# A two-layer hybrid trunk on one core: the third FFN column pair computed plainly, the norm's residual additions and sums of squares on VectorE, and a gate product placed ahead of the second gates

## The chip, the cores and the metric

The kernel runs on one core of a Trainium2 chip. The metric is the device time of one execution in microseconds (us). The engines are called as in the profile: PE is TensorE, PEld its weight loads, DVE is VectorE, ACT is ScalarE, POOL is GpSimd, SP is SyncE, which issues most loads.

## What is computed

A two-layer causal decoder trunk on 512 tokens of width 1024, float32 in and out. Layer 0 mixes with dilated attention and an S5 state-space block side by side; layer 1 mixes with a Griffin block (a convolution of width 4, block-diagonal gates, a linear recurrence, a GELU branch). Each mixer and each FFN stands between two RMS norms, and the second norm's output is added to the residual:

```python
def rms_norm(x, g):
    y = x32 * lax.rsqrt(jnp.mean(x32 * x32, axis=-1, keepdims=True) + NORM_EPS) * g
def swiglu(x, w_gate, w_up, w_down):
    return (jax.nn.silu(x @ w_gate) * (x @ w_up)) @ w_down
...
    x = x + rms_norm(mixer(rms_norm(x, g_mix_pre)), g_mix_post)
    x = x + rms_norm(swiglu(rms_norm(x, g_ffn_pre), ...), g_ffn_post)
```

(The last two lines are put in short form.) The FFN's hidden width is 2816, which is 22 blocks of 128 columns.

## The kernel before

The residual lies transposed in eight tiles `xT` of 128 features by 512 tokens. Products are made in float32 quality from three products of split operands: high by high, low by high, high by low (`mm3`, recorded as L170). Activations and weights are therefore split into a high part (a copy on ACT) and a low part (a subtraction on DVE); for weights these are L240 and L241, tiles `whi_*` and `wlo_*`.

**The norm.** `out_proj` (L416) makes an output projection and the two norms behind it. It is used three times: `mo0` (layer 0's mixer, ahead of its FFN), `fd0` (layer 0's FFN, ahead of layer 1's mixer) and `mo1` (layer 1's mixer, ahead of its FFN). `norm_half` (L478) handles one half of the tokens: `col_sums` adds squares over the features on PE (`cs`), `rstd_of` makes the reciprocal root, `bcast_row` spreads it over the partitions on PE (`bc`). Then for each of eight features: gain by row on DVE (L496, tile `o_*`), the residual addition (L500 on DVE for the first feature, L502 on POOL for the other seven), the high part `xh` on ACT (L503), the square `nsq` on ACT (L506), and later the low part `xl` on DVE (L491). `next_sums` (L470) adds these squares over the features on PE into `ns`, the sum for the next pre-norm: 32 matmuls of 128x1 per norm, which a trace shows as 64 rows. While a norm runs, `half_cols` (L555) already multiplies the first four columns of the next product, feature by feature (`mo0b`, `fd0b`, `mo1b`); one feature of one half is twelve 256-wide matmuls. The next pre-norm's factor is applied after the products, so it can come late.

**The FFN's columns.** `ffn_up` (L598) computes gate and up columns in pairs. Pairs 0 and 1 are the four plain columns begun in the norm. Pairs 2 to 21 use a Strassen-like scheme on 2x2 blocks, with 84 matmuls of 256 columns in place of 48 of 512. It needs transformed weights (`pair_weights`, L636: four additions, seven splits into high and low) and transformed activations `t1` to `t4` (L657 to L677, from `xa` and `xb`); `t1` is written over the second halves of `xh` and `xl`. The products are named by block, `f00b` to `f03b` in layer 0 and `f10b` to `f13b` in layer 1.

**Layer 1's mixer.** `odd_body` (L1484): four plain columns from the norm (`fd0b`), four more (`xbb`), the convolution (`xc`), gates (`rg` on PE, `gr` and `gi` on ACT, L1557), the recurrence (L1561; exponentials and roots on ACT, multiplications and a scan on DVE), and the branch `gate_product` (L1580, 24 matmuls of 512 columns each, tile `gg`), whose GELU times the recurrence gives `y1h` and `y1l` (L1596, L1597), the operands of `op_mo` in `mo1`. Lines 1601 to 1613 set the order of gates, recurrences and gate products.

**What sets the order.** A tile scheduler with a time model orders each engine's instructions; inside the norm `seq_of` and `pin` keep the written order of a half. A heap of generators (`start`, `step_one`, `tick`, `drain`) puts the norm's steps between matmuls by due times (NORM_CS, NORM_BC, NORM_F). Loads are issued on SP's queue in order, each when its buffer is free.

Of the kernel before, what the change touches and what calls it, by code (L numbers as in the profile page):

```python
# [19 lines left out]
P = 128  # L20
S = 512
# [73 lines left out]
def hybrid_trunk(  # L95
# [320 lines left out]
    def out_proj(wget, ks, yh, yl, pname, layer, nm, otile, gname, glayer, ntail, tail_alloc, early, eng0=None,  # L416
# [44 lines left out]
        xh, xl = xg_tiles(nm)  # L461
        acc2 = [None, None]
        ready.clear()
# [14 lines left out]
        def norm_half(h):  # L478
            def srcs(t):
                return [acc[:, t * P:(t + 1) * P], acc2[h][:, t % 2 * P:(t % 2 + 1) * P]]  # L480

            yield NORM_CS[h]
            cs = col_sums(srcs, 2 * h, 2, f"{nm}{h}")
            r = rstd_of(cs, 2, f"{nm}{h}", seq_of, None if eps is None else eps[:, 2 * h:2 * h + 2])
            yield NORM_BC[h]
            row = bcast_row(r, 2, f"{nm}{h}")
            late = []

            def split_lo():
                f = late.pop(0)  # L490
                seq_of(dve.scalar_tensor_tensor(xl[f][:, HS[h]], xT[f][:, HS[h]], col(gname, glayer * NF + f),  # L491
                                                xh[f][:, HS[h]].bitcast(F32), op0=ALU.mult, op1=ALU.subtract))

            for f in range(NF):
                oh, xf = o[f][:, HS[h]], xT[f][:, HS[h]]
                seq_of(dve.scalar_tensor_tensor(oh, oh, col(pname, layer * NF + f), row, op0=ALU.mult, op1=ALU.mult))  # L496
                if late and late[0] < max(NDVE, f - 1):
                    split_lo()
                if f < NDVE:
                    seq_of(dve.tensor_tensor(xf, xf, oh, op=ALU.add))  # L500
                else:
                    pool.tensor_tensor(xf, xf, oh, op=ALU.add)  # L502
                seq_of(act.activation(xh[f][:, HS[h]], xf, AF.Copy, scale=col(gname, glayer * NF + f)))  # L503
                if f % 2 == 0:
                    q = sb.tile([P, S], F32, tag="sqacc" if h else "sq", bufs=2, name=f"nsq_{nm}{h}{f}")
                seq_of(act.activation(q[:, HS[f % 2]], xf, AF.Square))  # L506
                late.append(f)
                if f % 2 and f > 1:
                    next_sums(h, (f - 3, f - 2), qlast)
                if f % 2:  # L510
                    qlast = q
                ready.update((h, q) for q in range(late[0]))
                yield NORM_F
            next_sums(h, (NF - 2, NF - 1), qlast)
            while late:
                split_lo()
            ready.update((h, q) for q in range(NF))
# [20 lines left out]
        drain()  # L538
        in_order[0] = False
        sets["main"].insert(0, nb)  # L540
        return xh, xl, (first, bs), nsum
# [7 lines left out]

    NFIRST = 4  # L550

    def first_cols(lst, nm, eng=None):
# [17 lines left out]

    def gemm_cols(lst, first, xh, xl, nm, evac):

# [7 lines left out]
        for i in range(NFIRST, len(lst)):  # L580
            w2 = wcols(lst[i][0], lst[i][1], NF, f"{nm}{i}")
            b = bank(f"{nm}b{i}")
            for k in range(NF):
                mm3(b, w2(k), xh[k], xl[k], k == 0, k == NF - 1)
            w2.free()
            evac(i, b)
# [11 lines left out]
    def ffn_up(layer, xh, xl, first, nsum, nm, hp):  # L598
# [32 lines left out]

        heads = gemm_cols(cols2[:NFIRST], first, xh, xl, nm, evac)
        next(heads)
# [15 lines left out]

        own = iter([*range(11, NH), 3, 4, 5, 6])  # L650
        for q in range(NFIRST // 2 + 3):
            retired.add((hp, f"hh{q}"))
        wa, wc, wd, wb = pair_weights(
            NFIRST // 2, lambda name: hp.tile([P, S], F32R, tag=f"hh{next(own)}", name=name), sb)


        t1 = [(xh[k][:, HS[1]], xl[k][:, HS[1]]) for k in range(HK)]  # L657
        th, tl = [], []
        for k in range(HK):
            a = hp.tile([P, S], F32, tag=f"hh{7 + k % 2}", name=f"xa_{nm}{k}")  # L660
# [3 lines left out]
            raw = Raw(4, HT, f"tr_{nm}{k}")  # L664
            (t2, t3), (t4, t0) = [(t[:, 0], t[:, 1]) for t in raw.parts]
            dve.tensor_tensor(t0, a[:, HS[1]], a[:, HS[0]], op=ALU.subtract)
# [4 lines left out]
            l = hp.tile([P, 3, HT], F32R, tag="tq", bufs=8, name=f"tl_{nm}{k}")  # L671
            for src, hi, lo in ((raw.parts[0], h[:, 0:2], l[:, 0:2]), (t4, h[:, 2], l[:, 2]), (t0, *t1[k])):
                act.activation(hi, src, AF.Copy)
                dve.tensor_tensor(lo, src, hi.bitcast(F32), op=ALU.subtract)
            raw.free()
            th.append(h)
            tl.append(l)  # L677
        for _ in heads:
            pass
        give([(hp, f"hh{q}") for q in range(7, NH)])  # L680
        X = {
# [11 lines left out]

        for n in range(NFIRST // 2, NH):
            if n > NFIRST // 2:
                for q in range(n + 3):
# [787 lines left out]
    def odd_body(xh, xl, first, nsum, lp):  # L1484
# [119 lines left out]
        recurrence(range(NF // 2))  # L1604
        gg += [gate_product(1), gate_product(2)]
        gates(2, last["sqrt"])
        gates(3, last["sqrt"])
        gg.append(gate_product(3))
        recurrence(range(NF // 2, NF))
# [61 lines left out]
```

## Time and profile before

| what | value |
|---|---|
| median of 3 runs | 1168.26 us (1167.83 to 1178.44) |
| the profiled execution | 1169.77 us, span 1167.7 us |
| mean granted PE clock of that execution | 0.990 |
| PE busy | 1131.7 us (97%), 7550 matmul rows |
| DVE busy | 876.8 us (75%), 1841 instructions |
| ACT busy | 626.6 us (54%) |
| POOL busy | 60.6 us (5%) |

Times in the rows are microseconds from the start of the span. A row of a chain gives start, length and the work that the end waited for. A row of a timeline gives start, length, engine, line, operation, output and inputs, and in brackets the idle time before it with what ended it. A row of the waits names the waiting engine and line, what released it, and the time in all, the number of waits and the longest. Groups of back-to-back instructions overlap in their ends, so the price of one in a row is the distance of starts rather than the length.

### The profile page before, as it was taken

To read this page: it belongs to the slowest core of one execution; us is meant where nothing else is said; L and a number is where in the kernel's file an instruction comes from. 1 tells how busy PE (TensorE), PEld (TensorE's weight loads), DVE (VectorE), ACT (ScalarE), POOL (GpSimd) and SP (SyncE) were. 2 spreads that over 40 slices of the span, in tenths; PEclk is the share of its full clock that TensorE was granted. 3 is DMA by queue.
4 is the path that set the end of the run, shared out by engine and by line. 5 is a ranking of instruction groups with operands and counts; after the bars stand their busy time and mean duration, and the time that the engine had idled before them with its cause. 6 is when DMAs were issued, how large, how long until landed. Compare 5 with 4: busy or idle time off the path is not lost.

```text
span 1167.7 us, 20255 instructions
## 1 busy us (share of the span) xinstructions
PE 1131.7 (97%) x7550; PEld 1013.2 (87%) x7550; DVE 876.8 (75%) x1841; ACT 626.6 (54%) x1290; POOL 60.6 (5%) x100
## 2 busy tenths in 40 slices
PE   6999899999999999999999999999999999999997
PEld 6877666889999999988889887889999999988886
DVE  7989675478999899882345887956999899984224
ACT  7556576357655555652244479744855455582221
POOL 1000010003000000000004000004000000000001
PEclk9999989999999999999999999999999999999999
DMA  8534410522333332423330323430253333334221
GB/s 211 144 117 134 108 45 1 172 64 63 93 109 100 101 99 83 125 92 96 121 100 1 106 86 98 126 109 1 77 146 95 101 109 91 90 119 126 91 63 72
DMA packets 165561, 113.45 MB, mean 97 GB/s; under 512 B 26852, under 2 KB 142296, under 8 KB 165464
## 3 DMA queue, kind: packets, MB, share of 16 engines
q1 hardware_dynamic: 162168, 109.95, 32.2%
q10 hardware_dynamic: 3040, 2.17, 0.7%
q8 instruction: 59, 0.97, 0.3%
q14 instruction: 38, 0.31, 0.1%
q0 software_dynamic: 256, 0.06, 0.0%
HBM read 103.75 MB, written 4.19 MB: 92 GB/s over the span
## 4 chain that ended last, share of the span: by engine, by line
PE 82%; DVE 5%; ACT 5%; DMA 4%; issue 2%; POOL 0%; ACTq 0%; DVEq 0%; POOLq 0%; SPq 0%
PE fo L170 10%; PE op_fd L170 10%; PE op_mo L170 6%; PE f00b L170 5%; PE f02b L170 5%; PE f01b L170 4%; PE f11b L170 4%; PE f10b L170 4%; PE f12b L170 4%; PE qkv L170 4%; PE gg L170 3%; PE f03b L170 2%; PE f13b L170 2%; PE mo1b L170 2%; PE mo0b L170 2%; PE xbb L170 2%
## 5 line engine op out<-in xcount | busy, mean ns | idle before, releaser
L241 DVE TENSOR_TENSOR wlo_fo<-wraw_fo,whi_fo 128x512 fp32r<-128x512 f32 x44 | 30.3, 691 | 63.8 <-PE fo L170 58.7
L170 PE MATMUL op_fd<-hi_f,whi_fd 128*128 128x512 f32 (+1 forms) x200 | 73.7, 369 | 0.0
L170 PE MATMUL op_fd<-lo_f,whi_fd 128*128 128x512 f32 (+1 forms) x200 | 73.4, 367 | 0.0
L170 PE MATMUL op_fd<-hi_f,wlo_fd 128*128 128x512 f32 (+1 forms) x200 | 73.0, 367 | 0.0
L170 PE MATMUL fo<-wlo_fo,hi_f 128*128 128x512 f32 x176 | 69.4, 394 | 0.0
L170 PE MATMUL fo<-whi_fo,lo_f 128*128 128x512 f32 x176 | 69.1, 394 | 0.0
L170 PE MATMUL fo<-whi_fo,hi_f 128*128 128x512 f32 x176 | 68.9, 396 | 0.0
L240 ACT ACTIVATE whi_fo<-wraw_fo 128x512 fp32r<-128x512 f32 x44 | 27.6, 631 | 70.6 <-DMA wraw_fo<-in_ffn_w_down_dram 43.4
L241 DVE TENSOR_TENSOR wlo_fd<-wraw_fd,whi_fd 128x512 fp32r<-128x512 f32 x44 | 30.1, 690 | 46.4 <-ACT whi_fd L240 42.5
L240 ACT ACTIVATE whi_fd<-wraw_fd 128x512 fp32r<-128x512 f32 x44 | 27.4, 629 | 54.7 <-DMA wraw_fd<-in_ffn_w_down_dram 33.8
L170 PEld LDWEIGHTS op_fd<-lo_f,whi_fd 128*128 128x128 f32 x200 | 37.7, 189 | 6.8
L170 PEld LDWEIGHTS op_fd<-hi_f,wlo_fd 128*128 128x128 f32 x200 | 37.7, 189 | 6.7
L170 PEld LDWEIGHTS op_fd<-hi_f,whi_fd 128*128 128x128 f32 x200 | 37.7, 189 | 6.6
L170 PE MATMUL qkv<-whi_qkv,xh_m 128*128 128x512 f32 x96 | 40.5, 427 | 0.0
L170 PEld LDWEIGHTS fo<-whi_fo,lo_f 128*128 128x128 f32 x176 | 33.1, 188 | 7.8
L170 PEld LDWEIGHTS fo<-whi_fo,hi_f 128*128 128x128 f32 x176 | 33.1, 188 | 7.7
L170 PEld LDWEIGHTS fo<-wlo_fo,hi_f 128*128 128x128 f32 x176 | 33.1, 188 | 7.5
L170 PE MATMUL qkv<-wlo_qkv,xh_m 128*128 128x512 f32 x96 | 38.3, 399 | 0.0
L170 PE MATMUL qkv<-whi_qkv,xl_m 128*128 128x512 f32 x96 | 38.0, 396 | 0.0
L644 DVE TENSOR_TENSOR wraw_s_f<-wraw_f,wraw_f 128x512 f32<-128x512 f32 x40 | 27.4, 684 | 11.4 <-DMA wraw_f<-in_ffn_w_up_dram 10.7
L241 DVE TENSOR_TENSOR wlo_mo<-wraw_mo,whi_mo 128x512 fp32r<-128x512 f32 x32 | 21.4, 686 | 14.5 <-ACT whi_mo L240 14.2
L645 DVE TENSOR_TENSOR wraw_t_f<-wraw_s_f,wraw_f 128x512 f32<-128x512 f32 x40 | 27.3, 682 | 6.0 <-DMA wraw_f<-in_ffn_w_gate_dram 6.0
(1974 smaller groups left out, 4297.8 us busy)
## 6 DMA issues: line engine op xcount, KB each, us to landing
wraw_f<-in_ffn_w_gate_dram SPq DMA_DIRECT2D x88, 256.0 KB, 3.1
wraw_f<-in_ffn_w_up_dram SPq DMA_DIRECT2D x88, 256.0 KB, 3.3
wraw_fd<-in_ffn_w_down_dram SPq DMA_DIRECT2D x44, 256.0 KB, 2.8
wraw_fo<-in_ffn_w_down_dram SPq DMA_DIRECT2D x44, 256.0 KB, 2.9
wraw_qkv<-in_ev_w_in_dram SPq DMA_DIRECT2D x24, 256.0 KB, 3.5
wraw_mo<-in_ev_w_out_dram SPq DMA_DIRECT2D x16, 256.0 KB, 4.3
wraw_xb<-in_od_w_in_dram SPq DMA_DIRECT2D x16, 256.0 KB, 2.8
wraw_gg<-in_od_w_in_dram SPq DMA_DIRECT2D x16, 256.0 KB, 2.8
```

The source lines that it names most:

```text
L170: self.pin(nc.tensor.matmul(o, lhsT=lhsT, rhs=rhs, start=start, stop=stop, **kw))
L240: act.activation(hi, src, AF.Copy)
L241: eng.tensor_tensor(lo, src, hi.bitcast(F32), op=ALU.subtract)
L644: dve.tensor_tensor(s1, a21, a22, op=ALU.add)
L645: dve.tensor_tensor(s2, s1, a11, op=ALU.subtract)
```

## The change

Three edits. First, a third pair of FFN columns is plain (`NPLAIN = 3`): `gemm_cols` gets two more columns, `f0b4` and `f0b5`, with weights `f0p4` and `f0p5`; the scheme begins with pair 3, and `t1` is put over `xh` and `xl` only after the plain columns. Second, in the norm all residual additions are on DVE, the squares go to a ring of half tiles, DVE adds them up, and PE makes four totals of 128x1 at the end. Third, the gate product of feature 3 is written ahead of the third and fourth gate blocks.

```diff
--- before.py
+++ after.py
@@ -459,7 +459,8 @@
             o.append(t)
         first = early()
         xh, xl = xg_tiles(nm)
-        acc2 = [None, None]
+        acc2, total = [None, None], [None, None]
+        on_dve = True
         ready.clear()


@@ -485,6 +486,11 @@
             yield NORM_BC[h]
             row = bcast_row(r, 2, f"{nm}{h}")
             late = []
+            if on_dve:
+
+                sq = [sb.tile([P, S], F32, tag="sqacc" if h else "sq", bufs=2, name=f"nsq_{nm}{h}{i}")
+                      for i in range(2)]
+                sq = [q[:, HS[i]] for q in sq for i in range(2)]

             def split_lo():
                 f = late.pop(0)
@@ -494,24 +500,33 @@
             for f in range(NF):
                 oh, xf = o[f][:, HS[h]], xT[f][:, HS[h]]
                 seq_of(dve.scalar_tensor_tensor(oh, oh, col(pname, layer * NF + f), row, op0=ALU.mult, op1=ALU.mult))
-                if late and late[0] < max(NDVE, f - 1):
+                if late and (on_dve or late[0] < max(NDVE, f - 1)):
                     split_lo()
-                if f < NDVE:
+                if on_dve or f < NDVE:
                     seq_of(dve.tensor_tensor(xf, xf, oh, op=ALU.add))
                 else:
                     pool.tensor_tensor(xf, xf, oh, op=ALU.add)
                 seq_of(act.activation(xh[f][:, HS[h]], xf, AF.Copy, scale=col(gname, glayer * NF + f)))
-                if f % 2 == 0:
-                    q = sb.tile([P, S], F32, tag="sqacc" if h else "sq", bufs=2, name=f"nsq_{nm}{h}{f}")
-                seq_of(act.activation(q[:, HS[f % 2]], xf, AF.Square))
                 late.append(f)
-                if f % 2 and f > 1:
-                    next_sums(h, (f - 3, f - 2), qlast)
-                if f % 2:
-                    qlast = q
+                if on_dve:
+                    seq_of(act.activation(sq[f % 3] if f else sq[3], xf, AF.Square))
+                    if f > 1:
+                        seq_of(dve.tensor_tensor(sq[3], sq[3], sq[(f - 1) % 3], op=ALU.add))
+                else:
+                    if f % 2 == 0:
+                        q = sb.tile([P, S], F32, tag="sqacc" if h else "sq", bufs=2, name=f"nsq_{nm}{h}{f}")
+                    seq_of(act.activation(q[:, HS[f % 2]], xf, AF.Square))
+                    if f % 2 and f > 1:
+                        next_sums(h, (f - 3, f - 2), qlast)
+                    if f % 2:
+                        qlast = q
                 ready.update((h, q) for q in range(late[0]))
                 yield NORM_F
-            next_sums(h, (NF - 2, NF - 1), qlast)
+            if on_dve:
+                seq_of(dve.tensor_tensor(sq[3], sq[3], sq[(NF - 1) % 3], op=ALU.add))
+                total[h] = sq[3]
+            else:
+                next_sums(h, (NF - 2, NF - 1), qlast)
             while late:
                 split_lo()
             ready.update((h, q) for q in range(NF))
@@ -537,6 +552,10 @@
         bs = half_cols(0, first, xh, xl, None, nm)
         drain()
         in_order[0] = False
+        if on_dve:
+            for t in range(NT):
+                pe.matmul(nsum[:, t:t + 1], lhsT=total[t // 2][:, t % 2 * P:(t % 2 + 1) * P], rhs=ones[:, 0:1],
+                          start=True, stop=True)
         sets["main"].insert(0, nb)
         return xh, xl, (first, bs), nsum

@@ -548,6 +567,7 @@
         return dve.scalar_tensor_tensor(l, src, g, h.bitcast(F32), op0=ALU.mult, op1=ALU.subtract)

     NFIRST = 4
+    NPLAIN = 3

     def first_cols(lst, nm, eng=None):
         return [wcols(w, c0, NF, f"{nm}{i}", base=sb, eng=eng) for i, (w, c0) in enumerate(lst[:NFIRST])]
@@ -568,7 +588,7 @@
                 tick()
         return bs

-    def gemm_cols(lst, first, xh, xl, nm, evac):
+    def gemm_cols(lst, first, xh, xl, nm, evac, ready_w=None):

         ws, bs = first
         half_cols(1, ws, xh, xl, bs, nm)
@@ -578,7 +598,7 @@
         for i in range(NFIRST):
             evac(i, bs[i])
         for i in range(NFIRST, len(lst)):
-            w2 = wcols(lst[i][0], lst[i][1], NF, f"{nm}{i}")
+            w2 = ready_w(i) if ready_w else wcols(lst[i][0], lst[i][1], NF, f"{nm}{i}")
             b = bank(f"{nm}b{i}")
             for k in range(NF):
                 mm3(b, w2(k), xh[k], xl[k], k == 0, k == NF - 1)
@@ -629,7 +649,7 @@
                 act.activation(env[n][1], b, AF.Copy)
                 gated(*env[n], n)

-        heads = gemm_cols(cols2[:NFIRST], first, xh, xl, nm, evac)
+        heads = gemm_cols(cols2[:2 * NPLAIN], first, xh, xl, nm, evac, lambda i: plain[i - NFIRST])
         next(heads)
         mid()

@@ -647,36 +667,47 @@
             dve.tensor_tensor(s4, a12, s2, op=ALU.subtract)
             return [Chunk(t, f"{nm}{n}{q}", alloc=alloc) for t, q in ((r0, "a"), (rs, "c"), (r1, "d"), (rt, "b"))]

-        own = iter([*range(11, NH), 3, 4, 5, 6])
-        for q in range(NFIRST // 2 + 3):
+        own = iter(range(11, NH))
+        for q in range(NPLAIN + 3):
             retired.add((hp, f"hh{q}"))
-        wa, wc, wd, wb = pair_weights(
-            NFIRST // 2, lambda name: hp.tile([P, S], F32R, tag=f"hh{next(own)}", name=name), sb)
+        plain = [Chunk(Raw(NF, P, f"{nm}p{i}", cols2[i][0][:, cols2[i][1]:cols2[i][1] + P].rearrange(
+            "(k p) n -> p k n", p=P), base=sb), f"{nm}p{i}",
+            alloc=lambda name: hp.tile([P, S], F32R, tag=f"hh{next(own)}", name=name))
+            for i in range(NFIRST, 2 * NPLAIN)]


         t1 = [(xh[k][:, HS[1]], xl[k][:, HS[1]]) for k in range(HK)]
         th, tl = [], []
+        z = Raw(HK, HT, f"tz_{nm}")
+        z0 = [z.parts[k // z.step][:, k % z.step] for k in range(HK)]
         for k in range(HK):
             a = hp.tile([P, S], F32, tag=f"hh{7 + k % 2}", name=f"xa_{nm}{k}")
             b = hp.tile([P, S], F32, tag=f"hh{9 + k % 2}", name=f"xb_{nm}{k}")
             act.activation(a, xT[k], AF.Copy, scale=col("g1", layer * NF + k))
             act.activation(b, xT[k + HK], AF.Copy, scale=col("g1", layer * NF + k + HK))
             raw = Raw(4, HT, f"tr_{nm}{k}")
-            (t2, t3), (t4, t0) = [(t[:, 0], t[:, 1]) for t in raw.parts]
+            (t2, t3), (t4, _) = [(t[:, 0], t[:, 1]) for t in raw.parts]
+            t0 = z0[k]
             dve.tensor_tensor(t0, a[:, HS[1]], a[:, HS[0]], op=ALU.subtract)
             dve.tensor_tensor(t3, b[:, HS[1]], a[:, HS[1]], op=ALU.subtract)
             dve.tensor_tensor(t2, b[:, HS[1]], t0, op=ALU.subtract)
             dve.tensor_tensor(t4, t2, b[:, HS[0]], op=ALU.subtract)
             h = hp.tile([P, 3, HT], F32R, tag="tq", bufs=8, name=f"th_{nm}{k}")
             l = hp.tile([P, 3, HT], F32R, tag="tq", bufs=8, name=f"tl_{nm}{k}")
-            for src, hi, lo in ((raw.parts[0], h[:, 0:2], l[:, 0:2]), (t4, h[:, 2], l[:, 2]), (t0, *t1[k])):
+            for src, hi, lo in ((raw.parts[0], h[:, 0:2], l[:, 0:2]), (t4, h[:, 2], l[:, 2])):
                 act.activation(hi, src, AF.Copy)
                 dve.tensor_tensor(lo, src, hi.bitcast(F32), op=ALU.subtract)
             raw.free()
             th.append(h)
             tl.append(l)
+        wa, wc, wd, wb = pair_weights(NPLAIN)
         for _ in heads:
             pass
+
+        for k in range(HK):
+            act.activation(t1[k][0], z0[k], AF.Copy)
+            dve.tensor_tensor(t1[k][1], z0[k], t1[k][0].bitcast(F32), op=ALU.subtract)
+        z.free()
         give([(hp, f"hh{q}") for q in range(7, NH)])
         X = {
             "11": [(xh[k][:, HS[0]], xl[k][:, HS[0]]) for k in range(HK)],
@@ -691,8 +722,8 @@
             for k in range(HK):
                 mm3(o[:, HS[0]], w2(k0 + k), x[k][0], x[k][1], k == 0 and not onto, k == HK - 1, skip_group_check=onto)

-        for n in range(NFIRST // 2, NH):
-            if n > NFIRST // 2:
+        for n in range(NPLAIN, NH):
+            if n > NPLAIN:
                 for q in range(n + 3):
                     retired.add((hp, f"hh{q}"))
                 places[:] = [p for p in places if p not in retired]
@@ -1602,10 +1633,9 @@
         gates(1)
         gg = [gate_product(0)]
         recurrence(range(NF // 2))
-        gg += [gate_product(1), gate_product(2)]
+        gg += [gate_product(1), gate_product(2), gate_product(3)]
         gates(2, last["sqrt"])
         gates(3, last["sqrt"])
-        gg.append(gate_product(3))
         recurrence(range(NF // 2, NF))
         for f in range(NF):
             gated(f, gg[f])
```

How the instructions move, at three places. The first is DVE in the first half of the norm `mo0`; `o_mo` is the projection, `xT` the residual, `xl` the low part, `nsq` the squares. Before:

```order
L496 SCALAR_TENSOR_TENSOR o_mo04_2932<-o_mo04_2932,cols_143,bc_mo00_3125 128x256
L491 SCALAR_TENSOR_TENSOR xl_mo02_2998<-xT_2_149,cols_143,xh_mo02_2990 128x256
L380 TENSOR_SCALAR rst_mo01_3216<-cs_mo01_3211 128x2
L496 SCALAR_TENSOR_TENSOR o_mo05_2934<-o_mo05_2934,cols_143,bc_mo00_3125 128x256
L491 SCALAR_TENSOR_TENSOR xl_mo03_2999<-xT_3_150,cols_143,xh_mo03_2991 128x256
L496 SCALAR_TENSOR_TENSOR o_mo06_2936<-o_mo06_2936,cols_143,bc_mo00_3125 128x256
L491 SCALAR_TENSOR_TENSOR xl_mo04_3000<-xT_4_151,cols_143,xh_mo04_2992 128x256
```

and in the change:

```order
L502 SCALAR_TENSOR_TENSOR o_mo05_2934<-o_mo05_2934,cols_143,bc_mo00_3125 128x256
L497 SCALAR_TENSOR_TENSOR xl_mo04_3000<-xT_4_151,cols_143,xh_mo04_2992 128x256
L506 TENSOR_TENSOR xT_5_152<-xT_5_152,o_mo05_2934 128x256
L514 TENSOR_TENSOR nsq_mo001_3129<-nsq_mo001_3129,nsq_mo000_3128 128x256
L502 SCALAR_TENSOR_TENSOR o_mo06_2936<-o_mo06_2936,cols_143,bc_mo00_3125 128x256
L497 SCALAR_TENSOR_TENSOR xl_mo05_3001<-xT_5_152,cols_143,xh_mo05_2993 128x256
L506 TENSOR_TENSOR xT_6_153<-xT_6_153,o_mo06_2936 128x256
L514 TENSOR_TENSOR nsq_mo001_3129<-nsq_mo001_3129 128x256
```

Two operations per feature have become four, and the split follows one feature behind the gain instead of two.

The second place is PE in the second half of `mo0`, where the squares' sums (`ns_mo`) stood among the first columns (`mo0b`). Before:

```order
L170 MATMUL mo0b0_3161<-xh_mo01_2989,whi_f00_0_2944 128x256
L474 MATMUL ns_mo0_3004<-ones_131,nsq_mo014_3351 128x1 x2
L170 MATMUL mo0b0_3161<-xh_mo01_2989,wlo_f00_0_2945 128x256
L170 MATMUL mo0b1_3162<-xh_mo01_2989,whi_f01_0_2956 128x256
L170 MATMUL mo0b1_3162<-xh_mo01_2989,wlo_f01_0_2957 128x256
L170 MATMUL mo0b2_3163<-xh_mo01_2989,whi_f02_0_2968 128x256
L474 MATMUL ns_mo0_3004<-ones_131,nsq_mo014_3351 128x1 x2
```

and in the change, at the end of that half, with the third plain pair (`f0b5`) behind it:

```order
L170 MATMUL mo0b3_3165<-xh_mo07_2995,wlo_f03_1_2985 128x256
L170 MATMUL ns_mo0_3004<-ones_131,nsq_mo011_3277 128x1 x2
L170 MATMUL mo0b0_3162<-xl_mo07_3003,whi_f00_1_2948 128x256
L170 MATMUL mo0b1_3163<-xl_mo07_3003,whi_f01_1_2960 128x256
L170 MATMUL mo0b2_3164<-xl_mo07_3003,whi_f02_1_2972 128x256
L170 MATMUL mo0b3_3165<-xl_mo07_3003,whi_f03_1_2984 128x256
L170 MATMUL f0b5_3654<-xh_mo00_2988,whi_f0p5_0_3495 128x512
L170 MATMUL f0b5_3654<-xl_mo00_2996,whi_f0p5_0_3495 128x512
```

A norm had eleven such groups of two or four matmuls; it now has two of two, one for each half.

The third place is PE in layer 1's mixer, at the last gate (`rg1_7`). Before:

```order
L170 MATMUL rg1_7_8616<-ch6_8220,wlo_rg3_1_8585 128x512
L170 MATMUL rg1_7_8616<-ch7_8269,whi_rg3_1_8584 128x512
L170 MATMUL rg1_7_8616<-cl7_8270,whi_rg3_1_8584 128x512
L170 MATMUL rg1_7_8616<-ch7_8269,wlo_rg3_1_8585 128x512
L170 MATMUL gg3_8638<-xh_fd00_7434,whi_gg3_0_8630 128x512
L170 MATMUL gg3_8638<-xl_fd00_7442,whi_gg3_0_8630 128x512
```

and in the change:

```order
L170 MATMUL gg4_8618<-xh_fd03_7354,whi_gg4_0_8610 128x512
L170 MATMUL rg1_7_8554<-ch6_8119,whi_rg3_1_8522 128x512
L170 MATMUL rg1_7_8554<-cl6_8120,whi_rg3_1_8522 128x512
L170 MATMUL rg1_7_8554<-ch6_8119,wlo_rg3_1_8523 128x512
L170 MATMUL rg1_7_8554<-ch7_8168,whi_rg3_1_8522 128x512
L170 MATMUL rg1_7_8554<-cl7_8169,whi_rg3_1_8522 128x512
L170 MATMUL rg1_7_8554<-ch7_8168,wlo_rg3_1_8523 128x512
L170 MATMUL gg4_8618<-xl_fd03_7362,whi_gg4_0_8610 128x512
```

All of `gg3` and ten matmuls of `gg4` now stand ahead of the last gate; behind it, ahead of `op_mo`, were 120 gate-product matmuls, and are 86.

## The prediction

> **What bounds the kernel now.** I read the page's busy times first, then the table of stretches, then the chain of waits inside the norms.
>
> ```profile
> PE 1131.7 (97%) x7550; PEld 1013.2 (87%) x7550; DVE 876.8 (75%) x1841; ACT 626.6 (54%) x1290; POOL 60.6 (5%) x100
> 257.30:291.90 34.60, 33.58 (x286) 33.29 (x285) 27.79 (x66) 24.62 (x56) 13.71 (x16) 1.00 0.19 53
> 617.10:654.90 37.80, 36.98 (x316) 36.73 (x315) 24.39 (x79) 16.21 (x39) 13.50 (x16) 1.00 0.11 32
> 788.60:826.90 38.30, 37.95 (x306) 37.83 (x306) 27.49 (x63) 23.34 (x54) 13.90 (x16) 0.94 0.15 42
> 320.00:460.00 140.00, 140.00 (x1179) 140.00 (x1178) 132.27 (x264) 73.94 (x152) 0.00 (x0) 1.00 0.35 101
> ```
>
> The columns of the stretches are the stretch and its length, busy time of PE, its weight loads, DVE, ACT and POOL, the granted clock, the DMA share and GB/s. PE is the bound, with two differences between stages. In the three norms with their first columns (rows 1 to 3 of the stretches: mo0, fd0, mo1) DVE has room, about 7 to 13 us in each. In the FFN's Strassen pairs (last row) PE never idles and DVE is busy 132.3 of 140 us, so work added to DVE there comes back as time almost at once. The question is how much DVE gets in the norms, and how much of that is left when the pairs begin.
>
> **Squares on TensorE.** The chain of waits through mo0 (240 to 300), mo1 (785 to 840) and fd0 (612 to 660) gives what the 128x1 sums cost on the path:
>
> ```profile
> by line: PE mo0b L170 37.6%; PE op_mo L170 11.1%; PE ns_mo L474 9.8%; PE f00b L170 7.6%; DMA wraw_f<-in_ffn_w_up_dram 6.3%; DVE wlo_f L241 3.0%; PE cs_mo L170 2.7%; issue 2.5%; PE f03b L170 2.2%; DVE oacc_mo L532 2.1%; PE f01b L170 2.0%; AC
> by line: PE mo1b L170 42.9%; PE op_mo L170 14.2%; PE ns_mo L474 9.5%; DMA wraw_f<-in_ffn_w_up_dram 5.8%; issue 4.1%; PE bc_mo L170 2.4%; DVE wraw_t_f L645 2.3%; DVE gt_f L627 2.2%; DVE tl_f L674 2.2%; PE cs_mo L170 2.1%; POOL xT L502 1.7%;
> by line: PE fd0b L170 42.5%; PE xbb L170 10.5%; PE ns_fd L474 8.4%; PE op_fd L170 8.2%; DVE o_fd L496 4.9%; POOL xT L502 3.8%; PE cs_fd L170 3.3%; ACT nsq_fd L506 3.2%; issue 2.7%; DVE xl_fd L491 2.5%; PE bc_fd L170 1.9%; ACT xh_fd L503 1.9
> L474 PE MATMUL ns_mo<-ones,nsq_mo x64: 164/250/271, 261.3 to 285.4; 128*128 128x1 f32 x64
> 275.71 0.79 PE ns_mo L474 x8
> 285.70 6.16 PE mo0b L170 x51
> 291.86 0.89 PE bc_f L170 x8
> ```
>
> 9.8% of 60 us is 5.9 us, 9.5% of 55 is 5.2, 8.4% of 48 is 4.0. Each norm has 64 trace rows, and eight of them take 0.79 us. The change leaves four totals, which are eight rows: 0.8 us stays. Gain 5.1 us in mo0, 4.5 in mo1 and at least 3.2 in fd0, which I treat with the odd layer below. A 128x1 group also delays the matmul behind it:
>
> ```profile
> 254.84 0.37 PE L170 MATMUL op_mo<-yh,whi_mo 128*128 128x256 f32 x1
> 255.04 0.28 PE L170 MATMUL op_mo<-yl,whi_mo 128*128 128x256 f32 x1
> ```
>
> The first 256-wide matmul behind such a group holds PE 0.20 us, where twelve in a row take 0.119 each (1.43 us at 299.78, shown below): 0.08 for each of about ten groups that go, so 0.85 us per norm, 1.7 for mo0 and mo1.
>
> **Waits in the norm.** From the table of what PE waits for (245 to 330, and 775 to 870), and DVE's rows at 250:
>
> ```profile
> PE cs_mo L170 <- DVE oacc_mo L532: 0.9, 1, 0.9
> PE cs_mo L170 <- ACT oqs_mo L530: 0.5, 1, 0.5
> PE cs_mo L170 <- DVE oacc_mo L532: 0.3, 1, 0.3
> PE ns_mo L474 <- ACT nsq_mo L506: 0.4, 1, 0.4
> PE ns_mo L474 <- ACT nsq_mo L506: 0.3, 1, 0.3
> 250.33 0.69 DVE L644 TENSOR_TENSOR wraw_s_f<-wraw_f,wraw_f 128x512 f32<-128x512 f32 x1 [2.25 <-DMA wraw_f<-in_ffn_w_up_dram]
> 250.94 0.42 DVE L532 TENSOR_TENSOR oacc_mo<-oacc_mo,oqs_mo 128x256 f32<-128x256 f32 x1
> ```
>
> An addition of the third pair's weights stands in DVE's order ahead of the square sums and waits 2.25 us for its load. In the changed order no weights of that pair stand there. Of the cs waits I take 1.5 us over mo0 and mo1 (0.9 + 0.5 in mo0, 0.3 and the same 0.5 in mo1, of which part may stay). The 0.7 us for the squares goes with the rows.
>
> **What DVE takes on.** Per norm 14 residual additions come from POOL (883 ns each there, 16 rows and 13.7 us of POOL, beside other work) and 14 running sums are new: 28 of 128x256. Prices by spacing of back-to-back rows:
>
> ```profile
> 253.18 0.74 DVE L529 TENSOR_TENSOR o_mo<-o_mo,op_mo 128x256 f32<-128x256 f32 x2
> 260.22 0.48 DVE L491 SCALAR_TENSOR_TENSOR xl_mo<-xT,cols,xh_mo 128x256 fp32r<-128x256 f32 x1
> 260.61 0.41 DVE L529 TENSOR_TENSOR o_mo<-o_mo,op_mo 128x256 f32<-128x256 f32 x1
> 263.13 0.51 ACT L503 ACTIVATE xh_mo<-xT,cols 128x256 fp32r<-128x256 f32 x1
> 263.55 0.40 ACT L506 ACTIVATE nsq_mo<-xT 128x256 f32<-128x256 f32 x1
> 280.37 0.68 DVE L241 TENSOR_TENSOR wlo_f02a<-wraw_f,whi_f02a 128x512 fp32r<-128x512 f32 x1
> 280.97 0.68 DVE L647 TENSOR_TENSOR wraw_s_f<-wraw_f,wraw_t_f 128x512 f32<-128x512 f32 x1
> 283.38 0.47 DVE L491 SCALAR_TENSOR_TENSOR xl_mo<-xT,cols,xh_mo 128x256 fp32r<-128x256 f32 x1
> 299.78 1.43 PE f00b L170 x12
> ```
>
> A two-tensor operation of 128x256 costs 0.33 us (0.74 less 0.41), one with a scalar 0.39 (260.22 to 260.61), a 128x512 one 0.60. One feature of a half is two of 0.39 (gain, split) and now two of 0.33: 1.45 us. PE needs twelve 256-wide matmuls for it: 1.43. So DVE and PE run level, and PE also has the sums over columns, the broadcast and the totals to do. I put the DVE work at zero on the path in mo0 and mo1. The bounds: 0 when the rows pack as above; and if each operation took its whole length (0.48, 0.48, 0.41, 0.41: 1.78 us), 16 steps would be 28.5 us against 23.2, some 5 us later per norm, 10 in all. The running sum adds a wait: it needs ACT's square of the feature before, and the next gain and split, for which PE waits, stand behind it on DVE. ACT's copy and square of a feature (starts 0.42 apart, 0.40 long) end about 1.3 us after its addition began (0.41 + 0.42 + 0.40 and hand-overs), and DVE comes to that sum 1.45 us after, so the wait is nothing, with little margin. I take the lower end because the rows show that packing in this very norm.
>
> The Trainium skill, "VectorE: DVE Perf Modes", section "The DRAIN you can't avoid", says that the next VectorE operation does not start until the pipe of the one before is empty, and adds that one which nothing holds starts earlier. Read strictly it gives 1.78 us a step and the rival below; the rows at 260.22 and 260.61 start 0.39 apart under a length of 0.48, so by the trace it is the exception that applies here.
>
> **The third pair plain, t1 and the gate order.** PE: the scheme takes 84 256-wide matmuls at 0.119 us, 10.0 us; the plain pair takes 48 512-wide ones.
>
> ```profile
> 744.45 26.54 PE op_mo L170 x114
> 716.80 27.66 PE gg L170 x120
> ```
>
> 27.66/120 is 0.2305, so 11.1 us: 1.1 more per layer, +2.1 in all. DVE saves seven 128x512 operations of weights per layer (four lo splits in place of four additions and seven splits) and about 1.2 us of combining: 5.4 us per layer. That is less than the 9.4 (28 x 0.334) that it takes on in the norm ahead. The first transform's split moves behind the plain pair, because it overwrites operands of that pair: four operations of 0.33 on DVE, beside the evacuations there. The gate order adds nothing by itself; its place is costed with the odd layer.
>
> **Where norm and pairs meet.** Before, DVE ends the last split at 283.9 and PE the first columns at 291.86 (rows at 283.38 and 291.86): a lead of 8 us, used for weights and transforms. Now both end together. From there DVE must do 2.4 us of lo splits, 9.1 of transforms (four tiles of four operations at 0.33, one at 0.60, one at 0.33), 6.6 of the fourth pair's weights and 2.4 of evacuations before everything is there, though the first products need some 13 to 15 us of it. PE has 0.5 left of the columns, 0.9 of the broadcast, and 11.1 of the plain pair: 12.5. The present stalls there:
>
> ```profile
> PE f02b L170 <- ACT whi_f03c L240: 1.0, 1, 1.0
> PE f01b L170 <- ACT pu_f L709: 1.0, 1, 1.0
> PE f11b L170 <- DVE tl_f L674: 1.1, 1, 1.1
> PE f13b L170 <- DVE ut_f L726: 0.5, 1, 0.5
> PE f10b L170 <- ACT pu_f L707: 0.5, 1, 0.5
> ```
>
> With the many short ones below the table's rows they come to some 6 us over the two layers (an estimate). They could all go (-6), or grow by the 8 us of DVE that must fit in 12.5, two or three a layer (+6). I take -2.
>
> **The odd layer.** fd0 gets the same relief on PE, but the layer behind it is tight: gg ends at 744.46 and op_mo begins at 744.45, without a gap, while y1l, its first operand, comes from a chain on ACT and DVE.
>
> ```profile
> 718.10 0.69 ACT L1557 ACTIVATE gi<-rg,cols 128x512 f32<-128x512 f32 x1
> 740.24 1.23 ACT L1596 ACTIVATE y1h<-gg 128x512 fp32r<-128x512 f32 x2 [0.80 <-DVE gg L1593]
> ```
>
> From the last gate (718.10) to the last of these y1h it takes 23.4 us, and about two more to the low parts. Before, 120 gate-product matmuls (27.66 us) cover that. In the changed order the fourth product, and ten matmuls of the fifth, stand ahead of the last gate, so 86 are left: 19.8 us. The last gate falls 34 x 0.2305 = 7.8 us later by that, some 5 us earlier by the norm: +3; and the cover is short by about 6. PE then waits at op_mo, and its gain is spent there. I put fd0 and the odd layer together at 0, between -6 (the whole relief of 5 and a little packing) and +4.
>
> **The sum.** -5.1 -4.5 (sums) -1.7 (breaks) -1.5 -0.7 (waits) +2.1 (plain pair) -2 (where they meet) +0 (odd) = -13.4. The profiled execution has 1169.77 us, its span 1167.7; the runs' median is 1168.26, 1.5 lower. 1169.8 - 13.4 - 1.5 gives **1154.9**.
>
> **The rivals.** (1) *The odd layer passes its gain on*: the recurrence moves ahead with PE, because ACT and DVE get their gates earlier as well. For it: in the first half of the gates ACT waits for PE. Against: the count of 86 above. It adds -5 to -6: **1149**. (2) *The norm is DVE's*: operations take their whole length, or wait for ACT's copies in between. Then the norms lose 10 of the gain and the meeting place gives nothing (+2): **1167**, no change; a state halfway gives 1161. For it: one step is 1.45 against 1.43, without margin. (3) *Slower: DVE's added work all comes back.* 3 x 9.4 less 2 x 5.4 is +17.4, and PE's savings only lengthen its waits: **1186**. It decides if PE waits for DVE from the first split of the norm to the last pair, so that DVE's idle 7 to 13 us of a norm cannot be filled, being spent waiting for rows of the same chain. Against: DVE's own waits in mo0 are mostly for PE and POOL, which go. (4) *The plain pair does not do what it says*, its weights being late: all four loads stand right behind the first columns' loads on SP's queue, and the transforms only need residual tiles, so I give it no share of its own; it would cost the 2 us of a load and look like rival 2.
>
> **How the numbers follow.** Forecast 0.45, rival 1 0.15, rival 2 with its halfway state 0.32, rival 3 0.08. About 1% is what the measurement tells from no change: below 1156.6 is faster, above 1179.9 slower. Rival 1 and most of the forecast, with the better part of the halfway state, make faster 0.58; the rest within 1% 0.35; slower 0.07. The range from 1147 to 1167 takes in both bounds of the odd layer and rival 2, and leaves out rival 3 and a little at either end.
>
> **What would show it.** Right: in mo0 and mo1 the time from the first column matmul to bc_f's place falls by 7 to 8 us; eight 128x1 rows a norm; DVE busy over 90% from first split to last with rows 0.33 and 0.39 apart; a wait of 4 to 7 us at op_mo in the odd layer. Wrong: waits of PE for xl in every step (rival 2), no wait at op_mo (rival 1), stalls of over 3 us at the first pair in the scheme, or PE idle inside the later pairs (rival 3).

## The result, and the profile after

The changed kernel takes 1162.43 us (median of 16 runs), the kernel before on the same chips 1171.28 us. The ratio is 0.9933, with a 95% interval from 0.9912 to 0.9953: faster by 0.7%, about 8 us (the two medians differ by 8.9). The forecast was a little over 13 us. Medians count every run, while the ratios leave out two that took far longer, one of this kernel (1367.8 us) and one with the gate order undone (3803.8 us). The profiled execution after the change took 1165.47 us (span 1163.7), some 3 us above its median, and the one before 1169.77, 1.5 us below; the stages below therefore sum to a smaller difference, 4 us, than the medians show.

The granted PE clock has to be read beside every time here. Among the runs of the kernel before, one took 1162.87 us at a mean granted clock of 0.998 and another 1173.38 us at 0.987, about 1 us for each 0.001. In the traces the clock drops to half for stretches of 3.4 to 10.2 us, at other places in each execution, and a stage in which PE works without a pause gets longer by half of such a stretch (an estimate from the clock alone). Where that touches a reading below, the text says so.

The first view is the table of stretches of the changed kernel: the three norms with their first columns, then the 40 us that follow the norms mo0 and mo1. The columns are as in the prediction.

```profile
255.60:284.60 29.00, 27.71 (x229) 27.07 (x227) 26.27 (x71) 17.16 (x41) 0.85 (x2) 1.00 0.07 19
613.80:645.60 31.80, 31.06 (x258) 30.66 (x257) 27.39 (x81) 15.47 (x38) 0.95 (x2) 1.00 0.13 36
783.50:818.60 35.10, 34.33 (x287) 33.92 (x286) 28.26 (x76) 18.37 (x44) 1.72 (x3) 1.00 0.06 16
284.60:324.60 40.00, 36.26 (x243) 32.49 (x242) 40.00 (x82) 30.72 (x62) 0.86 (x1) 1.00 0.40 113
818.60:858.60 40.00, 36.78 (x249) 33.11 (x248) 40.00 (x82) 31.14 (x63) 1.15 (x1) 1.00 0.39 113
```

The same 40 us of the kernel before:

```profile
291.90:331.90 40.00, 37.98 (x312) 37.15 (x311) 39.56 (x78) 27.59 (x57) 0.00 (x0) 1.00 0.34 97
827.20:867.20 40.00, 37.48 (x308) 36.63 (x307) 38.94 (x78) 28.68 (x58) 0.00 (x0) 1.00 0.36 100
```

The norm itself does what was expected of it: DVE fills 26.3 of 29 us in mo0 where it filled 27.8 of 34.6. Behind the norm DVE is busy in every microsecond, 40.00 of 40, in both layers, and PE is idle for 3.7 and 3.2 us, where it was idle for 2.0 and 2.5 before. DVE was nearly as full there before (39.56 and 38.94); what differs is how far ahead of PE it was when that stretch began: in mo0 its last split now ends at 282.5 and the first columns at 284.5, a lead of 2 us where it was 8.

The sums of squares on PE are gone from the path, as the group of their matmuls in the changed kernel shows (16 rows for mo0 and mo1 together, in place of 128):

```profile
L170 PE MATMUL ns_mo<-ones,nsq_mo x16: 164/250/250, 271.6 to 817.7; 128*128 128x1 f32 x16
```

In the chain of waits through mo0 (235 to 330) DVE's four operations have taken their place, back to back:

```profile
261.05 0.39 DVE o_mo L502
261.44 0.40 DVE xl_mo L497
261.83 0.33 DVE xT L506
262.17 0.34 DVE nsq_mo L514
262.50 0.39 DVE o_mo L502
...
268.16 3.57 PE mo0b L170 x30
271.73 0.34 PE ns_mo L170 x4
272.07 11.54 PE mo0b L170 x96
283.61 0.34 PE ns_mo L170 x4
283.94 0.58 PE mo0b L170 x4
284.52 5.84 PE f0b L170 x25
290.42 2.75 DMA wraw_f<-in_ffn_w_gate_dram
293.20 0.63 ACT whi_f05a L240
```

One feature takes 1.45 us on DVE (261.05 to 262.50). In the first half of the tokens (up to 267.3) it is mostly DVE that the chain follows; in the second half it is PE's columns, and the plain pair behind them. Then it goes through loads, ACT and DVE.

The stages, from the starts of PE's first and last matmul of each tile in the profiled executions (us; each stage begins where the one before it ends: norm mo0 at its first `cs`, norm fd0 at its first column matmul, norm mo1 at the last `op_mo`; a norm ends at its last column matmul, and the FFN columns of layer 1 at the last product of a pair):

| stage | before | after | difference | forecast |
|---|---|---|---|---|
| up to the norm mo0 | 253.3 | 252.1 | -1.2 | in the norms |
| norm mo0 | 38.3 | 32.1 | -6.2 | |
| norm mo1 | 32.5 | 26.3 | -6.2 | the two norms together -13.5 |
| FFN columns and down projection, layer 0 | 331.3 | 334.7 | +3.4 | |
| FFN columns, layer 1 | 209.9 | 212.6 | +2.7 | the two FFN stages together +0.1 |
| norm fd0 | 31.1 | 26.4 | -4.7 | |
| layer-1 mixer: columns, gates, gate products | 90.1 | 91.3 | +1.2 | |
| layer-1 mixer: op_mo | 50.4 | 55.3 | +4.9 | fd0 and mixer together 0 |
| last product and output | 123.7 | 125.7 | +2.0 | 0 |

Within layer 0's row the columns alone are 5.5 us longer (211.1 and 216.6) and the down projection is 2.1 shorter. Two rows hold half-clock time: before the change the granted clock was 0.95 in norm mo1 (about 1.7 us of its 32.5) and 0.97 in op_mo (1.7), after it 0.94 in op_mo (3.4). The columns of both layers ran at 1.00 in both executions.

### The profile page after: what moved, and what is told of

Read it like the earlier page. It is cut to its first block, busy times and chain, and to the rows that moved or that the text cites. A ratio compares the mean times of both kernels' runs of the same rounds, so it can differ in the third digit from the quotient of the medians.

```text
span 1163.7 us, 19752 instructions
## 1 busy us (share of the span) xinstructions
PE 1117.9 (96%) x7310; PEld 992.1 (85%) x7310; DVE 887.0 (76%) x1899; ACT 624.7 (54%) x1280; POOL 25.1 (2%) x58
## 4 chain that ended last, share of the span: by engine, by line
PE 76%; ACT 8%; DVE 7%; DMA 6%; issue 2%; SPq 0%; ACTq 0%; DVEq 0%; POOLq 0%; POOL 0%
PE fo L170 10%; PE op_fd L170 10%; PE op_mo L170 7%; PE f12b L170 4%; PE f10b L170 4%; PE f02b L170 4%; PE f11b L170 4%; PE f00b L170 4%; PE f01b L170 4%; PE qkv L170 3%; DMA wraw_f<-in_ffn_w_gate_dram 2%; PE f03b L170 2%; PE f13b L170 2%; PE xbb L170 2%; PE ub L170 1%
## 5 line engine op out<-in xcount | busy, mean ns | idle before, releaser
L240 ACT ACTIVATE whi_fd<-wraw_fd 128x512 fp32r<-128x512 f32 x44 | 27.6, 628 | 60.4 <-DMA wraw_fd<-in_ffn_w_down_dram 36.5
L170 PE MATMUL op_mo<-y1l,whi_mo 128*128 128x256 f32 (+1 forms) x88 | 30.8, 349 | 4.1 <-DVE y1l L1628 4.1
```

The costliest lines, as they stand in the source:

```text
L170: self.pin(nc.tensor.matmul(o, lhsT=lhsT, rhs=rhs, start=start, stop=stop, **kw))
```

## The experiments

Two theories of the missing gain were set against each other. **D**: DVE comes out of the norm without the lead that it used to have, is full for the following 50 to 60 us, and PE waits for what DVE owes it. **L**: the plain pair's weights and the kept transform hold buffers, so the weights of the next pairs are loaded late; the chain's row "290.42 2.75 DMA" and the table of what PE waits for, where the releasers are weights on ACT, speak for it:

```profile
PE f00b L170 <- ACT whi_f05a L240: 1.6, 1, 1.6
PE f00b L170 <- ACT pu_f L738: 1.1, 2, 0.6
PE f02b L170 <- ACT whi_f04c L240: 0.6, 1, 0.6
```

**The plain pair alone.**

```diff
-        on_dve = True
+        on_dve = False
```

(The gate order is also as before.)

> The third pair plain alone; norms and gate order as before. Theory D (DVE): the first pairs of the scheme stall because DVE enters them without a lead, packed back to back since the norm began. Here DVE keeps its lead of some 8 us and loses 5.4 us of work per layer, so PE's idle time between the norm and the second scheme pair falls under 2.5 us a layer (before 4.7 and 6.4 over the whole stage); with 1.1 us of extra matmuls per layer the time is 0 to 4 us below before, a ratio of 0.997 to 1.000. Theory L (loads): the plain pair's weights and the kept transform hold raw buffers, so the weights of the next pairs land late; then this kernel has the late loads and the 8 us of stalls of the whole change, without the norm's gain: 5 to 9 us above before, 1.004 to 1.008.

Measured: 1160.91 us against 1169.08, ratio 0.9936 [0.9910, 0.9961]. The stretches of this kernel behind its norms:

```profile
288.60:328.60 40.00, 40.00 (x294) 37.81 (x293) 39.69 (x76) 25.83 (x54) 0.00 (x0) 1.00 0.39 112
824.80:864.80 40.00, 40.00 (x293) 37.82 (x293) 40.00 (x76) 27.12 (x55) 0.00 (x0) 1.00 0.40 115
```

PE is busy in all 40 us, in both layers, although this kernel has the same plain weights and the same kept transform. Theory L fails here. The time fell further than either theory said: the plain pair alone brings as much as the whole change. The stages of the profiled execution do not place this gain well. In layer 1 the columns take 206.3 us in place of 209.9, in spite of 1.1 us more of matmuls; in layer 0 they take 213.8 in place of 211.1, of which 1.1 is the matmuls' price and about 1.7 a half-clock stretch of 3.4 us. A further 2.5 us are ahead of the first norm, where the code is the same and the granted clock was higher (0.99 against 0.97).

**The norm alone** (the norm's code from the change, all else from the kernel before).

> The norm's additions and square sums on DVE alone; pairs and gate order as before. Both theories: the norms mo0 and mo1 are 6 to 7 us shorter each. Theory D: DVE lacks 9.4 us of lead and has all of the third pair's weights and transforms to do at once, so each FFN stage is 5 to 8 us longer than before and the gain is gone: ratio 0.997 to 1.003. Theory L: without the plain pair the loads come as before, the FFN stages keep their length, and the time falls by 11 to 14 us: ratio 0.988 to 0.991, better than the whole change.

Measured: 1170.35 us against 1169.08, ratio 1.0008 [0.9986, 1.0031]. Behind the norms:

```profile
288.90:328.90 40.00, 33.63 (x256) 31.26 (x257) 40.00 (x86) 30.51 (x61) 3.27 (x1) 1.00 0.37 105
825.10:865.10 40.00, 34.47 (x258) 32.49 (x258) 39.67 (x86) 30.72 (x63) 2.60 (x1) 0.96 0.37 105
```

PE is idle 6.4 and 5.5 us with DVE full or nearly so. The norms are 2.9 and 4.6 us shorter, the columns 7.1 and 5.5 us longer (218.2 and 215.4). The norms gained less than the 6 to 7 us expected; in mo0 the granted clock was 0.90, which is about 3.4 us of that. The 0.96 in the last row is about 1.7 us of the columns. So the norm's edit by itself is worth nothing, and it is not the plain pair that makes the stalls; the plain pair is what keeps them small.

**The gate order undone.**

```diff
-        gg += [gate_product(1), gate_product(2), gate_product(3)]
+        gg += [gate_product(1), gate_product(2)]
         gates(2, last["sqrt"])
         gates(3, last["sqrt"])
+        gg.append(gate_product(3))
```

> The whole change with gate product 3 back behind the second gates. If the chain of ACT and DVE from the last gate to the first operands of op_mo sets that start, the wait of 5 us at op_mo only moves to the gates: within 1 us of the whole change. If the new order makes the wait (rival), the recurrence begins some 5 us earlier here and most of the wait goes: 3 to 5 us below the whole change, 0.990 of before or less.

Measured: 1163.10 us against 1169.08, ratio 0.9940 [0.9914, 0.9966], the whole change's 0.9933 within the noise. What PE waits for between 645 and 790, first in the whole change (the table of 600 to 790), then in this kernel (645 to 760):

```profile
PE op_mo L170 <- DVE y1l L1628: 4.1, 1, 4.1
PE rg L170 <- ACT gr L1588: 1.5, 1, 1.5
PE op_mo L170 <- ACT y1h L1627: 1.0, 1, 1.0
```

```profile
PE rg L170 <- ACT gr L1588: 6.5, 1, 6.5
```

The waits are of one size, 6.6 us in the first (5.1 of it at op_mo) and 6.5 in the second, all at the gates. The order decides only where PE waits. That fits a chain of gates, recurrence and GELU on ACT and DVE that does not move ahead with PE; no run changed that chain itself.

**The running sums on POOL.**

```diff
-                        seq_of(dve.tensor_tensor(sq[3], sq[3], sq[(f - 1) % 3], op=ALU.add))
+                        pool.tensor_tensor(sq[3], sq[3], sq[(f - 1) % 3], op=ALU.add)
```

(and the same for the last of them.)

> The whole change, but the running sums of squares (14 of 128x256 per norm) on POOL instead of DVE. Theory D: DVE gets back 4.7 us per norm, so its lead at the pairs is some 4 us and the stalls there fall by 3 to 4 us a layer: 5 to 8 us below the whole change, ratio 0.986 to 0.989 of before. Theory L: no load moves, within 1.5 us of the whole change (0.992 to 0.995). If POOL's operations lengthen DVE's beside them (before, splits took 0.54 us beside POOL's additions and 0.48 without), the norm itself gets up to 2 us longer.

Measured: 1161.93 us against 1169.08, ratio 0.9930 [0.9900, 0.9961]: by the medians no difference from the whole change, which taken alone would speak for L. But these seven runs had a lower mean clock (0.9896, against 0.9921 in the whole change). Where the clocks are alike, at 0.992 and 0.993, the three runs here took 1156.7 to 1158.0 us and the five of the whole change 1161.7 to 1163.8: some 5 us less, which is what D expected. With so few runs this is a hint and no proof. The stretches of the norms mo0 and mo1, and what DVE waits for in mo0 (255 to 283.5):

```profile
255.00:283.20 28.20, 27.43 (x229) 26.97 (x227) 23.10 (x56) 16.60 (x40) 13.89 (x15) 1.00 0.07 20
782.00:815.00 33.00, 32.31 (x271) 32.12 (x271) 25.03 (x60) 17.49 (x42) 14.06 (x16) 1.00 0.06 17
```

```profile
DVE xl_mo L497 <- ACT xh_mo L509: 3.4, 11, 1.2
DVE oacc_mo L547 <- ACT oqs_mo L545: 1.4, 2, 0.9
```

DVE got its 4.7 us back and spent most of them waiting: with one operation less per step, each split comes to its turn before ACT's copy is there, and eleven such waits take 3.4 us. Little of the lead was gained, so this run tests D weakly: in layer 0 norm and columns take 246.0 us in place of 248.7, in layer 1 240.4 in place of 238.9 (with a half-clock stretch of 3.4 us in it). The run with a lead for DVE, below, was built on this.

**DVE in mo0 and mo1 only; fd0's norm and the gate order as before.**

```diff
-        on_dve = True
+        on_dve = nm != "fd0"
```

> The plain pair, with the norm's additions and sums on DVE in mo0 and mo1 only; fd0's norm and the gate order as before. By the stages of the runs so far the layer-1 mixer with its norm takes 170.8 us where both are as before (in the kernel with the plain pair alone) and 173.0 in the whole change: 2 us below the whole change, ratio 0.990 to 0.993. If fd0's relief is worth its 4 us after all (rival), it is 3 to 5 us above the whole change.

Measured: 1157.32 us against 1168.65, ratio 0.9892 [0.9857, 0.9927], some 5 us below the whole change. Norm fd0, gates and op_mo take 34.1 + 89.8 + 47.0 = 170.9 us, against 173.0 in the whole change and 171.6 before (6.8 us of each of the first two sums, and 3.4 of the third, ran at half clock). Moving fd0's work to DVE, with the gate order, was a small loss of about 2 us; the rest lies in stages that this edit does not touch.

**A lead for DVE**: as that kernel, with the running sums on POOL and the splits two features behind.

```diff
-                if late and (on_dve or late[0] < max(NDVE, f - 1)):
+                if late and late[0] < max(NDVE, f - 1):
```

> As the kernel before in this list, with the running sums in mo0 and mo1 on POOL and each split two features behind its gain, as in the kernel before the change, so that DVE does not wait for ACT's copies in the norm. Theory D: DVE's step is 1.11 us against PE's 1.43; it enters the pairs with a lead of 4 to 6 us, stalls at the first pairs fall under 2 us a layer (after the change 5.9 and 5.4), and norm plus pairs take 243 us in layer 0 and 235 in layer 1, against 248.7 and 238.9 in the whole change: ratio 0.982 to 0.987, faster than both kernels. If the stalls stay (rival: loads or ACT set them), 0.990 to 0.993.

Measured: 1152.61 us against 1168.65, ratio 0.9853 [0.9824, 0.9883], faster than both kernels; the profiled execution took 1152.45 us, on the median. In its norms, and behind them:

```profile
252.00:281.60 29.60, 28.50 (x236) 27.87 (x235) 27.32 (x65) 19.53 (x46) 13.37 (x16) 1.00 0.08 23
777.00:808.90 31.90, 31.59 (x266) 31.39 (x265) 28.34 (x68) 20.19 (x47) 13.55 (x17) 1.00 0.09 25
281.60:321.60 40.00, 38.30 (x269) 35.28 (x269) 40.00 (x80) 28.83 (x58) 0.00 (x0) 1.00 0.41 116
808.90:848.90 40.00, 37.67 (x259) 34.31 (x259) 40.00 (x80) 27.76 (x57) 0.00 (x0) 1.00 0.36 100
```

DVE no longer waits for ACT's copies in mo0 (1.1 us in the whole change), so it does FFN work already in the norm. PE's idle time behind the norms falls from 3.7 and 3.2 us to 1.7 and 2.3. Norm and columns together take 245.0 us in layer 0 and 234.6 in layer 1, against 248.7 and 238.9 in the whole change and 248.0 and 238.9 in the kernel just above, from which this one differs only by the sums on POOL and the later splits. At like clocks (0.993) its runs took 1152.6 to 1153.6 us and those of the whole change 1161.7 to 1162.6. Stalls under 2 us a layer, as D said, were not reached in layer 1.

**Work added to DVE** (sixteen additions of 128x256 per layer that nobody reads, beside the norm's end and the transforms).

```diff
+        tax = sb.tile([P, S], F32, tag="sq", bufs=2, name=f"tax_{nm}")
+        for j in range(16):
+            dve.tensor_tensor(tax[:, HS[j % 2]], xT[j % NF][:, HS[0]], xT[j % NF][:, HS[1]], op=ALU.add)
         wa, wc, wd, wb = pair_weights(NPLAIN)
```

> The whole change with sixteen more additions of 128x256 on DVE per layer, 5.3 us whose results nobody reads, in and right behind the norms mo0 and mo1. Theory D (DVE is the pacemaker from the norm to the fifth or sixth pair): each layer gets 4 to 6 us longer, 8 to 12 in all, ratio 1.000 to 1.004 of before. Theory L (loads set the stalls, DVE has room): at most 3 us longer.

Measured: 1172.18 us against 1168.65, ratio 1.0020 [0.9996, 1.0043]: 10 us above the whole change (0.0087 of 1169) for 10.7 us of work on DVE (32 x 0.334). Behind the norms:

```profile
286.80:326.80 40.00, 34.73 (x194) 30.22 (x194) 38.78 (x81) 28.85 (x56) 4.21 (x1) 0.87 0.33 93
827.60:867.60 40.00, 34.15 (x210) 29.80 (x209) 39.78 (x83) 29.94 (x57) 4.21 (x1) 0.96 0.35 101
```

PE is idle for 5.3 and 5.9 us, 4.2 more in all than in the whole change. Norm and columns grew by 7.3 us in layer 0 (33.8 + 222.2) and 5.3 in layer 1 (27.6 + 216.6), but the clock column shows that the whole 10 us cannot be put down to DVE: at 0.87 and 0.96, up to 6.8 us of this growth is half-clock time. The twelve runs had a mean clock of 0.986 against 0.992. Where the clocks are alike, at 0.991 and 0.992, two runs here took 1166.8 and 1167.8 us and three of the whole change 1162.2 to 1165.5, 3.5 us less on the mean. So between 3.5 and 10 us of the 10.7 came back as time; whether the added work itself brings the lower clock is not shown. The lower bound is hardly above the 3 us that L allowed, so this run alone does not decide.

D's direction is shown by three runs (the plain pair alone, the norm alone, the lead), the added work agrees with it, and its rate is known only roughly. With the plain pair's run L is out as a cause of its own. The waits of SP's queue in the whole change (240 to 335) fit late loads as an effect of a late DVE, since two of the longer ones end on DVE's transforms (by the order of the semaphores, which does not prove it):

```profile
SPq L216 <- DVE wraw_tz_f L691: 8.3, 1, 8.3
SPq L216 <- DVE wraw_tr_f L694: 6.6, 1, 6.6
```

## Why the prediction was wrong, point by point

**The squares on PE, the breaks and the waits.** Right in size, with some luck. The forecast for mo0 and mo1 was 13.5 us; the two norms with the start of the first are 13.6 us shorter (6.2 + 6.2 + 1.2). About 1.7 of these are the lower clock (0.95) in mo1 before the change, so at one clock it is nearer 12.

**DVE's added work at zero on the path.** Right inside the norm, where the rows pack to 1.45 us a feature as they were priced; none took its whole length, and rival 2 (a norm paced by whole lengths) did not occur.

**Where norm and pairs meet: the step that failed.** The prediction put -2 there and named the range from -6 to +6. Together with the plain pair's +2.1 its sum for the two FFN stages was +0.1; they came out 6.1 longer. So the term itself measured about +4.0, inside its range and 6 us from the value taken, which is the largest part of what the stages fall short of the forecast (9.4 us). It counted 20.5 us of DVE work against 12.5 of cover and saw that the lead of 8 us was gone, but then treated DVE as late only for the first products. DVE has no idle time for some 40 us more, and PE's idle time in them grew by 1.7 and 0.7 us; the remaining 1.6 of the 4.0 are not placed. The work added in the norm, 9.4 us, is larger than the 5.4 that the plain pair saves: 4.0 a layer, 8 in all, of which half came back. With the norm's edit alone it is 9.4 a layer, and the columns grew by 7.1 and 5.5 us (1.7 of these the clock's). The runs with the lead and with work added to DVE moved the stalls as a late DVE would.

**The plain pair at +2.1 on PE.** Right as a price and wrong as a value. Alone it is a gain of about 7.5 us in this kernel (0.64% of 1169). The likely reason, argued here and not shown by the stages, is that in front of pairs in which DVE is full the 5.4 us of DVE work that it saves a layer are worth more than the 1.1 us of matmuls that it costs. The prediction gave it no gain beyond a part of the stalls.

**fd0 and the odd layer at 0.** Nearly right: 1.4 us longer, which the lower clock in op_mo (some 1.7 us more of it than before) would account for. PE waits 5.1 us at op_mo, as forecast (4 to 7). Rival 1, a mixer that moves ahead with PE, did not occur; with the order undone the wait only moved to the gates.

**The last stage.** Not foreseen: PE waits 1.6 us for ACT ahead of the last product, and the stage is 2.0 longer. The stage has two lengths in these kernels and follows none of the edits: 125.7 to 125.9 in the whole change, with the gate order undone and with the lead, and 123.4 to 123.8 in all the others. It may be chance in the order that the scheduler finds; the cause stays open.

**Rival 3**, DVE's work all coming back, was priced at +17.4 because the norms were given no gain. Its mechanism is the one that acted, for the stages behind mo0 and mo1: there it returned about 4 us of a gain of 13.6 (the plain pair's price took 2.1 more), and with the norm's edit alone all of it.

## What to carry to other kernels

An engine with idle time in one stage is not free there if the next stage is bound by it: its idle time is often a lead, and the lead is spent first. Before giving it work, count it over both stages, up to the point where the second stage has a slack of its own, and put a price on what is left; here about half of it came back as time, and by the medians of one run nearly all. And an edit that lowers the load of that engine can be worth more than its cost on the engine that shows 97% busy; of three edits measured together, time each alone. Compare runs at like granted clocks: a difference of 0.005 was worth some 5 us here.

## What the runs showed of the hardware

Beside additions on POOL, some of DVE's operations get longer in the same norm. First the changed kernel, then the kernel with the lead (252 to 284 in both):

```profile
L497 DVE SCALAR_TENSOR_TENSOR xl_mo<-xT,cols,xh_mo 128x256 fp32r<-128x256 f32 x16 | 7.6, 478 | 1.1 <-ACT xh_mo L509 1.1
L502 DVE SCALAR_TENSOR_TENSOR o_mo<-o_mo,cols,bc_mo 128x256 f32<-128x256 f32 x16 | 7.6, 473 | 0.1
```

```profile
L497 DVE SCALAR_TENSOR_TENSOR xl_mo<-xT,cols,xh_mo 128x256 fp32r<-128x256 f32 x16 | 9.4, 597 | 0.0
L502 DVE SCALAR_TENSOR_TENSOR o_mo<-o_mo,cols,bc_mo 128x256 f32<-128x256 f32 x16 | 7.5, 471 | 0.5 <-PE bc_mo L170 0.4
```

The split takes 597 ns in place of 478 while POOL adds squares (some 0.8 to 0.9 us each); the gain, with operands of the same shape, stays at 471 to 473. POOL's additions are not the whole of it: in the kernel that has the same sums on POOL but splits one feature behind the gain, the split takes 488 ns. The residual additions take 454 ns there and 452 with the lead, in place of 416. What makes these operations longer is not told apart by these runs.

DVE starts operations closer together than they are long, behind the norm too:

```profile
288.97 0.42 DVE L693 TENSOR_TENSOR wraw_tr_f<-xb_f,wraw_tz_f 128x256 f32<-128x256 f32 x1
289.31 0.68 DVE L241 TENSOR_TENSOR wlo_f03a<-wraw_f,whi_f03a 128x512 fp32r<-128x512 f32 x1
289.91 0.69 DVE L241 TENSOR_TENSOR wlo_f03d<-wraw_f,whi_f03d 128x512 fp32r<-128x512 f32 x1
```

An operation of 128x256 is followed after 0.34 us and one of 128x512 after 0.60, where the lengths are 0.42 and 0.68.
